# One pool for weights, parts and sums, and a deeper look-ahead in the MLP of a two-layer trunk

## The chip, the cores and the metric

The kernel runs on one core of a Trainium2 chip. The metric is device time in microseconds of one execution, the median of several runs. The engines are called as in the profile: PE (TensorE's matmuls), PEld (its weight loads), DVE (VectorE), ACT (ScalarE), POOL (GpSimd) and SP (SyncE, which here only issues loads and stores). Each engine takes its instructions in the order in which the program has them, and waits on semaphores for the others.

## The reference, cut to what matters

256 tokens of width 2048 go through two layers. Each has attention (main heads and four heads against a memory), an output projection, and a squared-ReLU MLP of width 8192; before the second layer shared keys and values are projected once. Everything is in float32. The change lies in how the weights are brought to TensorE, above all in the MLP:

```python
def sq_relu_mlp(h, g, w_in, w_out):
    return jnp.square(jax.nn.relu(rms_norm(h, g) @ w_in)) @ w_out

def reference(x, mem, ...):
    h = x
    for layer in range(DEPTH):
        ...
        h = h + jnp.concatenate([y_main, y_mem], axis=-1) @ w_o[layer]
        h = h + sq_relu_mlp(h, norm_mlp[layer], w_mlp_in[layer], w_mlp_out[layer])
    return h
```

## The kernel before, in words

**Weights as a stream.** All weights are read once, as a list `stream` of 932 units in the order of their use. A unit is 128 x 1024 float32, 4 KB in each partition. `prepare` (L248) makes one ready: SP loads it into a tile `raw` (L269, L261 or L226), ACT casts it to `hi` in the format fp32r (L189, L265 or L243), and DVE subtracts, `lo = raw - hi` (L192, L266 or L244). TensorE then multiplies with hi and lo apart: hi by hi, hi by lo and lo by hi give a product that is close to float32. `weights` (L273) hands out the next unit, and before that prepares as many as `AHEAD` says: the unit that is handed out and three more.

**Pools.** `raws` has 6 buffers, `his` 4, `los` 5, all of 4 KB in a partition. A fourth pool `grp` has 13 buffers of the same size, for what lives longer: heads, sums, tiles of the residual stream, copies.

**The MLP.** `mlp` (L1022) goes over four chunks of 2048 of the 8192 hidden features, and over the output in column groups. `mlp_steps` writes out the order of work from the table `TURNS`:
- U: one up tile, `features_major` (L408), two units: 16 matmuls of 512 columns with hi and then 16 of 256 columns with lo, into one bank. Then `up` (L1220): ACT copies one half of the bank to `low` (L467), DVE adds the other half (`up`, L1228), and `finish` multiplies by the root (L1210), squares on ACT (L1213) and splits the result into hi and lo (L1160 on ACT, L1161 on DVE) in the tile `hid`. After every second tile of those that a sevenfold product reads, `block_sums` also makes sums of 128x128 blocks on DVE (L1191 to L1194) and splits them into `s_w` and `s_x`.
- S: a sevenfold pair, `Group.seven` (L1130): a 2x2 block product with seven multiplications in place of eight. It takes two loads, left and right, and four units of the stream. Its 21 matmuls of 512 columns go in four steps of 6, 3, 6 and 6, one for each unit; within a product they read hi, lo, hi.
- A and B: direct units, 12 matmuls each.

There are 41 pairs S in a layer, 82 in all, and all but two follow an up tile U at once.

**The four units of a pair.** `prepare_seven` (L220) is called once for each. Step 0 loads both sides and splits the left one. Step 1 splits one block of the right side, half a unit (128x512). Step 2 forms two sums in place on DVE (L238, L239) and splits the right side. Step 3 forms two more (L241, L242) and splits the left side.

**What sets the order.** TensorE's instructions keep the order of the program. Those of ACT, DVE, POOL and SP are put in an order by a scheduler when the kernel is built; it also decides which free buffer of a pool a tile gets. Once built, each engine's order is fixed, and an instruction that waits holds up all that stand behind it on its engine.

Of the kernel before, what the change touches and what calls it, by code (L numbers as in the profile page):

```python
# [9 lines left out]
F32 = mybir.dt.float32  # L10
# [6 lines left out]
P = 128  # L17
# [18 lines left out]

WO_ORDER = [12, 13, 14, 15] + list(range(12))
AHEAD = 3

FIRST = 4  # L40

# [79 lines left out]
def trunk(  # L121
# [17 lines left out]
    nc = Engines(tc)  # L139

    const = ctx.enter_context(tc.tile_pool(name="const", bufs=1))
    raws = ctx.enter_context(tc.tile_pool(name="raws", bufs=6))
    his = ctx.enter_context(tc.tile_pool(name="his", bufs=4))
    los = ctx.enter_context(tc.tile_pool(name="los", bufs=5))
    acts = ctx.enter_context(tc.tile_pool(name="acts", bufs=2))
    grp = ctx.enter_context(tc.tile_pool(name="grp", bufs=13))
    wide = ctx.enter_context(tc.tile_pool(name="wide", bufs=7))
    nar = ctx.enter_context(tc.tile_pool(name="nar", bufs=6))
    tiny = ctx.enter_context(tc.tile_pool(name="tiny", bufs=4))
# [31 lines left out]

    stream = []
    prepared = deque()
    state = {"next": 0}

    def parts(raw, hi, lo, shared=False):

# [6 lines left out]
    def prepare_pair(load, split):  # L194


        i = state["next"]
        state["next"] = i + 2
        units = [
            (  # L200
                stream[n],
                raws.tile([P, 1024], F32, name=f"raw{n}", tag="raw"),
                his.tile([P, 1024], F32R, name=f"hi{n}", tag="hi"),
                los.tile([P, 1024], F32R, name=f"lo{n}", tag="lo"),
            )
            for n in (i, i + 1)
        ]
        for k2 in range(2):
            c = slice(512 * k2, 512 * (k2 + 1))
            load(i + k2)  # L210
            for src, raw, _, _ in units:
                nc.sync.dma_start(raw[:, c], src[:, c])
        for k2 in range(2):
            c = slice(512 * k2, 512 * (k2 + 1))
            split(i + k2)
            for _, raw, hi, lo in units:
                parts(raw[:, c], hi[:, c], lo[:, c], i == 0 and k2 == 0)
        prepared.extend((hi, lo) for _, _, hi, lo in units)

    def prepare_seven(i, seven):  # L220

        if seven.step == 0:
            seven.raw = []
            for n, ap in enumerate(seven.sides):
                raw = raws.tile([P, 1024], F32, name=f"raw{i}_{n}", tag="raw")
                nc.sync.dma_start(raw[:].rearrange("p (o x) -> p o x", o=4), ap)  # L226
                seven.raw.append(raw[:].rearrange("p (o k n) -> p k o n", o=4, k=2))
        left, right = seven.raw
        b11, b21, b12, b22 = left[:, 0], left[:, 1], right[:, 0], right[:, 1]
        hi = his.tile([P, 1024], F32R, name=f"hi{i}", tag="hi")  # L230
        lo = los.tile([P, 1024], F32R, name=f"lo{i}", tag="lo")
        hi4 = hi[:].rearrange("p (k o n) -> p k o n", o=4, k=2)
        lo4 = lo[:].rearrange("p (k o n) -> p k o n", o=4, k=2)
        src = left if seven.step in (0, 3) else right
        if seven.step == 1:
            src, hi4, lo4 = b22, hi4[:, 0], lo4[:, 0]
        elif seven.step == 2:
            nc.vector.tensor_tensor(b22, b22, b12, op=ALU.subtract)  # L238
            nc.vector.tensor_tensor(b12, b12, b11, op=ALU.subtract)  # L239
        elif seven.step == 3:  # L240
            nc.vector.tensor_tensor(b11, b22, b11, op=ALU.add)  # L241
            nc.vector.tensor_tensor(b21, b21, b11, op=ALU.subtract)  # L242
        nc.scalar.copy(hi4, src)  # L243
        nc.vector.tensor_tensor(lo4, src, hi4.bitcast(F32), op=ALU.subtract)  # L244
        seven.step += 1
        prepared.append((hi, lo))

    def prepare():  # L248
        i = state["next"]
        if i >= len(stream):  # L250
            return
        state["next"] = i + 1
        if isinstance(stream[i], Sevenfold):
            prepare_seven(i, stream[i])
            return
        raw = raws.tile([P, 1024], F32, name=f"raw{i}", tag="raw")
        hi = his.tile([P, 1024], F32R, name=f"hi{i}", tag="hi")
        lo = los.tile([P, 1024], F32R, name=f"lo{i}", tag="lo")
        if isinstance(stream[i], Gathered):

            nc.sync.dma_start(raw[:].rearrange("p (o x) -> p o x", o=4), stream[i].ap)  # L261
            turned = raw[:].rearrange("p (o k n) -> p k o n", o=4, k=2)
            hi4 = hi[:].rearrange("p (k o n) -> p k o n", o=4, k=2)
            lo4 = lo[:].rearrange("p (k o n) -> p k o n", o=4, k=2)
            nc.scalar.copy(hi4, turned)  # L265
            nc.vector.tensor_tensor(lo4, turned, hi4.bitcast(F32), op=ALU.subtract)  # L266
            prepared.append((hi, lo))
            return
        nc.sync.dma_start(raw[:], stream[i])  # L269
        parts(raw[:], hi[:], lo[:])  # L270
        prepared.append((hi, lo))

    def weights(held=0):  # L273

        while len(prepared) < AHEAD + 1 - held and state["next"] < len(stream):
            prepare()
        return prepared.popleft()

# [146 lines left out]
    def two_tiles(act, evacuates, order=tuple(range(KT))):  # L425

        banks = [ps_mm.tile([P, 512], F32, name="acc", tag="acc") for _ in range(2)]
        units = [weights(held=i) for i in range(4)]
        kinds = [(wide_ones, 0), (narrow_ones, 1)]
        if width["last"] == "narrow":  # L430
            kinds.reverse()
        for i, (ones_of, part) in enumerate(kinds):
            if i == 1 and part == 1:

                prepare()
            for b in range(2):
                for h in range(2):
                    ones_of(
                        banks[b], units[2 * b + h][part], act, order[8 * h : 8 * h + 8],
                        i == 0 and h == 0, i == 1 and h == 1,  # L440
                    )
                    if i == 1 and len(prepared) < AHEAD + 1:
                        prepare()
                if i == 1:
                    evacuates[b](banks[b])
                slot()
# [575 lines left out]
    def mlp(l, xg_, sq, h, done):  # L1022
# [62 lines left out]
        class Group:  # L1085
# [19 lines left out]
            def add(self, q, a, w):  # L1105
# [13 lines left out]
                    self.staged.append((dst, copy[:]))  # L1119
                else:  # L1120
                    whole, i = place(q, self.n)
                    first = whole.name not in self.copies
                    if first:
                        self.copies[whole.name] = heads4("copy")
                    copy = self.copies[whole.name]
                    nc.scalar.copy(copy[:, i * 512 : (i + 1) * 512], src)  # L1126
                    if not first:
                        nc.gpsimd.dma_start(out=whole[:], in_=copy[:], accum_op=ALU.add)  # L1128
# [73 lines left out]
            return [a11, first[0] if whole else s1, s2, s3, s4]  # L1202

        began = clock["slot"]
        chunks = [({}, {}) for _ in range(NCH)]

        def finish(c, f):
# [50 lines left out]
        for c, n, kind, i in mlp_steps(l):  # L1258
# [19 lines left out]
            else:  # L1278
                groups[c, n].direct(i, "AB".index(kind) + 1)
        c = NCH - 1  # L1280
        start_side(merge_first())

        def down(o, bank):
# [222 lines left out]
```

## Time and profile before

| what | value |
|---|---|
| median of 3 runs | 2206.19 us (2205.29 to 2206.84) |
| the profiled execution's own time | 2207.83 us |
| its span, first to last instruction | 2206.0 us |
| busy: PE, PEld, DVE, ACT, POOL | 98%, 83%, 80%, 59%, 11% |
| first MLP, 460 to 1125 us: PE, DVE, ACT busy | 648.75, 584.89, 413.60 us |
| second MLP, 1510 to 2206 us: PE, DVE, ACT busy | 673.66, 593.92, 421.62 us |
| loads of w_down, w_up, w_in: issue to landing, median | 6.6, 4.5, 3.8 us |

How to read the rows of the profile. A group's row gives the line, the engine, the operation, `out<-in` by the program's names, the shapes and the count, then busy time and the mean of one in ns, then the idle time of the engine just ahead of them and what ended it. A row of the timeline gives start, duration, engine, line and operation, and in brackets the idle time before it with its releaser. A matmul of 512 columns shows as 0.39 us, but the next one starts 0.23 us after it, since they overlap. A row of the windows gives a stretch of time, its length, the busy time of PE, PEld, DVE, ACT and POOL with the count of instructions, the clock that TensorE was granted as a share of the full one, and what the DMA engines did.

### The profile page before, as it was taken

The page shows a single profiled execution, that of the slowest core. Times are in us where ns is not written, and L with a number is a line of the kernel's source. Part 1 is how long each engine was busy: PE and PEld are TensorE (multiplying, and loading weights), DVE is VectorE, ACT ScalarE, POOL GpSimd, SP SyncE. Part 2 cuts the span into 40 slices and gives each one's busy share as a digit, 9 for nine tenths or more (in the row PEclk, how much of TensorE's full clock was granted, in tenths as well). Part 3 has the DMA queues.
Part 4 walks back from the last instruction along what each step waited for, and adds up shares of the span by engine and source line. Part 5 has one row for each costly group of instructions (what it writes and reads, how often), then busy time and mean ns, then how long its engine had stood idle before and what let it go on. Part 6 is the DMA issues. An engine that isn't in the chain of part 4 may idle for free.

```text
span 2206.0 us, 30581 instructions
## 1 busy us (share of the span) xinstructions
PE 2163.0 (98%) x11002; PEld 1837.8 (83%) x11002; DVE 1759.5 (80%) x2637; ACT 1295.6 (59%) x1932; POOL 241.9 (11%) x275
## 2 busy tenths in 40 slices
PE   9999999999999999999999999999999999999999
PEld 8888888887887887887878888888788788888787
DVE  7778886679889898897985556567989989888886
ACT  7644445556666665666545446655666566666653
POOL 0110103500000000000050112361000000000000
PEclk9999999999999999999999999999999999999999
DMA  9655556656665867867757663566676576776874
GB/s 331 209 162 186 177 176 207 213 174 192 196 212 173 238 197 215 238 209 231 218 173 210 183 198 118 153 211 191 172 216 190 185 227 203 221 216 213 245 213 124
DMA packets 220809, 441.94 MB, mean 200 GB/s; under 512 B 14065, under 2 KB 145137, under 8 KB 220657
## 3 DMA queue, kind: packets, MB, share of 16 engines
q1 hardware_dynamic: 212592, 410.63, 60.4%
q0 software_dynamic: 7488, 27.27, 5.0%
q8 instruction: 86, 1.41, 0.3%
q10 hardware_dynamic: 576, 2.10, 0.3%
q14 instruction: 67, 0.54, 0.1%
HBM read 415.82 MB, written 7.34 MB: 192 GB/s over the span
## 4 chain that ended last, share of the span: by engine, by line
PE 85%; DMA 7%; DVE 5%; ACT 2%; issue 1%; SPq 0%; ACTq 0%
PE acc L92 80%; DMA raw<-in_w_down 6%; DVE lo L244 2%; PE yp L92 1%; PE accs L92 1%; PE tp L92 1%; ACT hi L243 1%; PE s L92 1%; PE z L92 1%; ACT hi L265 1%; DVE lo L192 0%; DVE raw L242 0%; DVE raw L241 0%; ACT copy L1126 0%; DVE raw L239 0%
## 5 line engine op out<-in xcount | busy, mean ns | idle before, releaser
L192 DVE TENSOR_TENSOR lo<-raw,hi 128x1024 fp32r<-128x1024 f32 (+1 forms) x524 | 640.5, 1237 | 192.7 <-ACT hi L189 168.4
L189 ACT CAST hi<-raw 128x1024 fp32r<-128x1024 f32 (+1 forms) x524 | 539.2, 1045 | 302.7 <-PE acc L92 248.6
L92 PE MATMUL acc<-mlpx,hi 128*128 128x512 f32 x2048 | 485.3, 390 | 0.0
L243 ACT CAST hi<-raw 128x1024 fp32r<-128x1024 f32 x328 | 309.1, 944 | 280.9 <-DVE raw L239 153.3
L92 PE MATMUL acc<-hi,hid 128*128 128x512 f32 x1308 | 452.2, 393 | 3.8 <-ACT hi L243 2.4
L92 PEld LDWEIGHTS acc<-mlpx,hi 128*128 128x128 f32 x2048 | 384.3, 188 | 80.4 <-DVE up L1228 0.3
L244 DVE TENSOR_TENSOR lo<-raw,hi 128x1024 fp32r<-128x1024 f32 x328 | 354.1, 1087 | 93.3 <-ACT hi L243 90.1
L92 PEld LDWEIGHTS acc<-hi,hid 128*128 128x128 f32 x1308 | 247.2, 189 | 55.2 <-ACT hi L243 4.8
L92 PE MATMUL acc<-lo,hid 128*128 128x512 f32 x654 | 258.7, 396 | 14.8 <-DVE lo L244 14.8
L92 PEld LDWEIGHTS acc<-mlpx,lo 128*128 128x128 f32 x2048 | 261.5, 191 | 9.2
L92 PE MATMUL acc<-mlpx,lo 128*128 128x256 f32 x2048 | 264.9, 283 | 0.0
L92 PE MATMUL acc<-hi,xg 128*128 128x512 f32 x640 | 208.5, 398 | 0.0
L92 PEld LDWEIGHTS acc<-lo,hid 128*128 128x128 f32 x654 | 123.8, 189 | 42.6 <-DVE lo L244 21.2
L92 PEld LDWEIGHTS acc<-hi,xg 128*128 128x128 f32 x640 | 120.2, 188 | 24.6
L1128 POOL DMA_DIRECT2D e<-copy x16 | 13.8, 862 | 1021.1 <-ACT copy L1126 1019.7
L92 PE MATMUL acc<-lo,xg 128*128 128x512 f32 x320 | 124.8, 390 | 0.6 <-DVE lo L192 0.6
L92 PE MATMUL acc<-hi,s_w 128*128 128x512 f32 x328 | 121.2, 407 | 2.0 <-ACT hi L243 2.0
L467 ACT COPY low<-acc 128x256 f32<-128x256 f32 x188 | 69.4, 369 | 88.1 <-PE acc L92 86.8
L92 PE MATMUL acc<-y,hi 128*128 128x512 f32 x512 | 119.9, 391 | 0.0
L266 DVE TENSOR_TENSOR lo<-raw,hi 128x1024 fp32r<-128x1024 f32 x84 | 102.9, 1236 | 16.9 <-ACT hi L265 16.1
L265 ACT CAST hi<-raw 128x1024 fp32r<-128x1024 f32 x84 | 88.3, 1059 | 39.0 <-PE acc L92 33.6
L92 PEld LDWEIGHTS acc<-y,hi 128*128 128x128 f32 x512 | 95.0, 188 | 19.0
(232 smaller groups left out, 2775.9 us busy)
## 6 DMA issues: line engine op xcount, KB each, us to landing
raw<-in_w_up SPq DMA_DIRECT2D x256, 512.0 KB, 4.5
raw<-in_w_down SPq DMA_DIRECT2D x256, 512.0 KB, 6.6
raw<-in_w_in SPq DMA_DIRECT2D x80, 512.0 KB, 3.8
raw<-in_w_o SPq DMA_DIRECT2D x64, 512.0 KB, 4.2
raw<-in_w_mem SPq DMA_DIRECT2D x28, 512.0 KB, 5.8
raw<-in_w_kv_v SPq DMA_DIRECT2D x24, 512.0 KB, 4.3
raw<-in_w_kv_k SPq DMA_DIRECT2D x24, 512.0 KB, 4.4
raw<-in_w_q SPq DMA_DIRECT2D x24, 512.0 KB, 4.3
```

Of the source, the lines that this page charges most:

```text
L92: return self._tc.keep_in_program_order(fn(*args, **kwargs))
L189: nc.scalar.copy(hi[:, :n], raw[:, :n])
L192: nc.vector.tensor_tensor(lo, raw, hi.bitcast(F32), op=ALU.subtract)
L243: nc.scalar.copy(hi4, src)
L244: nc.vector.tensor_tensor(lo4, src, hi4.bitcast(F32), op=ALU.subtract)
L265: nc.scalar.copy(hi4, turned)
L266: nc.vector.tensor_tensor(lo4, turned, hi4.bitcast(F32), op=ALU.subtract)
L467: nc.scalar.copy(low[:], bank[:, T:])
L1128: nc.gpsimd.dma_start(out=whole[:], in_=copy[:], accum_op=ALU.add)
```

## The change

Three things. The three pools `raws`, `his` and `los` are given up, and `grp` grows from 13 to 28 buffers, the same memory (6 + 4 + 5 + 13): any unit's raw, hi or lo, and any sum or copy, takes any buffer that is free. In the MLP, up to its last chunk's direct part, `weights` keeps four units ahead in place of three. And in `prepare_seven` the two sums of step 3 are formed in step 2, behind the first two. The lines of the changed file are up to three lower than before (L243 becomes L240, L244 L241, L467 L464, L1228 L1227, L238 to L242 become L236 to L239). A fourth edit only changes the key of a dictionary from a tile's name to the tile itself.

```diff
+AHEAD_MLP = 4
...
-    raws = ctx.enter_context(tc.tile_pool(name="raws", bufs=6))
-    his = ctx.enter_context(tc.tile_pool(name="his", bufs=4))
-    los = ctx.enter_context(tc.tile_pool(name="los", bufs=5))
     acts = ctx.enter_context(tc.tile_pool(name="acts", bufs=2))
-    grp = ctx.enter_context(tc.tile_pool(name="grp", bufs=13))
+    grp = ctx.enter_context(tc.tile_pool(name="grp", bufs=28))
...
-    state = {"next": 0}
+    state = {"next": 0, "ahead": AHEAD}
...
-        raw = raws.tile([P, 1024], F32, name=f"raw{i}", tag="raw")
-        hi = his.tile([P, 1024], F32R, name=f"hi{i}", tag="hi")
-        lo = los.tile([P, 1024], F32R, name=f"lo{i}", tag="lo")
+        raw = grp.tile([P, 1024], F32, name=f"raw{i}", tag="g4")
+        hi = grp.tile([P, 1024], F32R, name=f"hi{i}", tag="g4")
+        lo = grp.tile([P, 1024], F32R, name=f"lo{i}", tag="g4")
...
         elif seven.step == 2:
             nc.vector.tensor_tensor(b22, b22, b12, op=ALU.subtract)
             nc.vector.tensor_tensor(b12, b12, b11, op=ALU.subtract)
-        elif seven.step == 3:
             nc.vector.tensor_tensor(b11, b22, b11, op=ALU.add)
             nc.vector.tensor_tensor(b21, b21, b11, op=ALU.subtract)
...
-        while len(prepared) < AHEAD + 1 - held and state["next"] < len(stream):
+        while len(prepared) < state["ahead"] + 1 - held and state["next"] < len(stream):
...
         began = clock["slot"]
+        state["ahead"] = AHEAD_MLP
...
         c = NCH - 1
+        state["ahead"] = AHEAD
         start_side(merge_first())
```

The change also gives the scheduler other buffers to work with, so the order on the engines moves. Two places show it, both for one pair in the first MLP, units 188 to 191 of the stream, which follows the up tile of units 186 and 187. `low` and `up` are that up tile's last steps and read its finished bank (`acc`).

DVE before, from the lo of the pair's first unit (188) to that of the fourth (191):

```order
L244 TENSOR_TENSOR lo188_5126<-raw188_0_5121,hi188_5125 128x1024
L244 TENSOR_TENSOR lo189_5137<-raw188_1_5123,hi189_5136 128x512
L238 TENSOR_TENSOR raw188_1_5123<-raw188_1_5123 128x4x128
L239 TENSOR_TENSOR raw188_1_5123<-raw188_1_5123,raw188_0_5121 128x4x128
L241 TENSOR_TENSOR raw188_0_5121<-raw188_1_5123,raw188_0_5121 128x4x128
L242 TENSOR_TENSOR raw188_0_5121<-raw188_0_5121 128x4x128
L244 TENSOR_TENSOR lo190_5181<-raw188_1_5123,hi190_5180 128x1024
L1228 TENSOR_TENSOR up_5174<-acc_5135,low_5172 128x256
L244 TENSOR_TENSOR lo191_5187<-raw188_0_5121,hi191_5186 128x1024
```

DVE now, the same stretch:

```order
L241 TENSOR_TENSOR lo188_5111<-raw188_0_5106,hi188_5110 128x1024
L1227 TENSOR_TENSOR up_5173<-acc_5130,low_5171 128x256
L241 TENSOR_TENSOR lo189_5121<-raw188_1_5108,hi189_5120 128x512
L1209 SCALAR_TENSOR_TENSOR up_5173<-up_5173,ri_mlp0_4400 128x256
L236 TENSOR_TENSOR raw188_1_5108<-raw188_1_5108 128x4x128
L237 TENSOR_TENSOR raw188_1_5108<-raw188_1_5108,raw188_0_5106 128x4x128
L1159 TENSOR_TENSOR hid0_4166<-up_5173,hid0_4166 128x256
L238 TENSOR_TENSOR raw188_0_5106<-raw188_1_5108,raw188_0_5106 128x4x128
L239 TENSOR_TENSOR raw188_0_5106<-raw188_0_5106 128x4x128
L241 TENSOR_TENSOR lo190_5132<-raw188_1_5108,hi190_5131 128x1024
L241 TENSOR_TENSOR lo191_5180<-raw188_0_5106,hi191_5179 128x1024
```

`up` has moved from behind the third unit's lo to a place ahead of the second unit's, and with it the four sums and three lo now stand behind it.

ACT before, from the hi of unit 188 to that of unit 191:

```order
L243 CAST hi188_5125<-raw188_0_5121 128x1024
L243 CAST hi189_5136<-raw188_1_5123 128x512
L243 CAST hi190_5180<-raw188_1_5123 128x1024
L467 COPY low_5172<-acc_5135 128x256
L243 CAST hi191_5186<-raw188_0_5121 128x1024
```

ACT now:

```order
L240 CAST hi188_5110<-raw188_0_5106 128x1024
L464 COPY low_5171<-acc_5130 128x256
L240 CAST hi189_5120<-raw188_1_5108 128x512
L1212 ACTIVATE up_5173<-up_5173 128x256
L1158 CAST hid0_4166<-up_5173 128x256
L240 CAST hi190_5131<-raw188_1_5108 128x1024
L240 CAST hi191_5179<-raw188_0_5106 128x1024
```

The copy `low` has moved from behind the third unit's hi to a place ahead of the second unit's. Of the 82 pairs, 76 stand like this now, `low` ahead of the second hi and `up` ahead of the second lo; in the other kinds the steps of `block_sums` lie between the sums too. Before, the `up` of the tile just ended stood ahead of no second lo; at 12 pairs it stood ahead of the third lo, among the sums.

More of the change, by code (lines that the diff above doesn't have):

```diff
@@ L201, in prepare_pair @@
                 stream[n],
-                raws.tile([P, 1024], F32, name=f"raw{n}", tag="raw"),
-                his.tile([P, 1024], F32R, name=f"hi{n}", tag="hi"),
-                los.tile([P, 1024], F32R, name=f"lo{n}", tag="lo"),
+                grp.tile([P, 1024], F32, name=f"raw{n}", tag="g4"),
+                grp.tile([P, 1024], F32R, name=f"hi{n}", tag="g4"),
+                grp.tile([P, 1024], F32R, name=f"lo{n}", tag="g4"),
             )
@@ L224, in prepare_seven @@
             for n, ap in enumerate(seven.sides):
-                raw = raws.tile([P, 1024], F32, name=f"raw{i}_{n}", tag="raw")
+                raw = grp.tile([P, 1024], F32, name=f"raw{i}_{n}", tag="g4")
                 nc.sync.dma_start(raw[:].rearrange("p (o x) -> p o x", o=4), ap)
@@ L255, in prepare @@
             return
-        raw = raws.tile([P, 1024], F32, name=f"raw{i}", tag="raw")
-        hi = his.tile([P, 1024], F32R, name=f"hi{i}", tag="hi")
-        lo = los.tile([P, 1024], F32R, name=f"lo{i}", tag="lo")
+        raw = grp.tile([P, 1024], F32, name=f"raw{i}", tag="g4")
+        hi = grp.tile([P, 1024], F32R, name=f"hi{i}", tag="g4")
+        lo = grp.tile([P, 1024], F32R, name=f"lo{i}", tag="g4")
         if isinstance(stream[i], Gathered):
@@ L441, in two_tiles @@
                     )
-                    if i == 1 and len(prepared) < AHEAD + 1:
+                    if i == 1 and len(prepared) < state["ahead"] + 1:
                         prepare()
@@ L1121, in add @@
                     whole, i = place(q, self.n)
-                    first = whole.name not in self.copies
+                    key = id(whole)
+                    first = key not in self.copies
                     if first:
-                        self.copies[whole.name] = heads4("copy")
-                    copy = self.copies[whole.name]
+                        self.copies[key] = heads4("copy")
+                    copy = self.copies[key]
                     nc.scalar.copy(copy[:, i * 512 : (i + 1) * 512], src)
```

## The prediction

> **What bounds the kernel now.** I read the page first, then the busy time by stage, the waits of TensorE, and at last the timeline around a pair of weight units that waits.
>
> ```profile
> PE 2163.0 (98%) x11002; PEld 1837.8 (83%) x11002; DVE 1759.5 (80%) x2637; ACT 1295.6 (59%) x1932; POOL 241.9 (11%) x275
> ...
> 460.00:1125.00 665.00, 648.75 (x3268) 547.79 (x3267) 584.89 (x851) 413.60 (x611) 24.78 (x29) 0.99 0.70 207
> ...
> 1510.00:2206.00 696.00, 673.66 (x3411) 569.19 (x3409) 593.92 (x861) 421.62 (x621) 18.96 (x24) 0.99 0.67 201
> ...
> PE acc L92 <- DVE lo L244: 23.1, 27, 1.6
> PE acc L92 <- ACT hi L243: 9.1, 13, 2.7
> ```
>
> The first row is busy time over the whole span: TensorE is the bound, and idle for 43 us of the 2206. The next two are the two MLPs (span, then busy PE, PEld, DVE, ACT, POOL): 16.3 and 22.3 of those 43 us lie there, while DVE is busy for 88% and 85%. The last two say for what: 40 waits, 32.2 us, for the two halves of the weights of the sevenfold pairs (L243 and L244; a pair is four units of the stream). So time can only be won or lost at one question: are the hi and lo of a pair's four units ready when TensorE comes to them?
>
> A pair that waits, with its rows on TensorE, ACT and DVE in turn (start, duration, last the idle time and its releaser):
>
> ```profile
> 501.94 0.40 PE L92 MATMUL acc<-hi,hid 128*128 128x512 f32 x1
> 502.17 0.40 PE L92 MATMUL acc<-lo,hid 128*128 128x512 f32 x1
> ...
> 504.01 0.39 PE L92 MATMUL acc<-hi,hid 128*128 128x512 f32 x1
> 505.09 0.50 PE L92 MATMUL acc<-lo,hid 128*128 128x512 f32 x1 [0.70 <-DVE lo L244]
> ...
> 506.14 0.40 PE L92 MATMUL acc<-hi,s_w 128*128 128x512 f32 x1
> 506.78 0.50 PE L92 MATMUL acc<-hi,s_w 128*128 128x512 f32 x1 [0.24 <-ACT hi L243]
> 508.04 0.50 PE L92 MATMUL acc<-lo,s_w 128*128 128x512 f32 x1 [0.76 <-DVE lo L244]
> ```
>
> ```profile
> 502.14 0.37 ACT L467 COPY low<-acc 128x256 f32<-128x256 f32 x1 [1.00 <-PE acc L92]
> 502.41 1.05 ACT L243 CAST hi<-raw 128x1024 fp32r<-128x1024 f32 x1
> ...
> 505.68 1.05 ACT L243 CAST hi<-raw 128x1024 fp32r<-128x1024 f32 x1 [1.32 <-DVE raw L242]
> ```
>
> ```profile
> 502.55 0.42 DVE L1228 TENSOR_TENSOR up<-acc,low 128x256 f32<-128x256 f32 x1 [0.60 <-ACT low L467]
> 502.89 0.68 DVE L241 TENSOR_TENSOR raw<-raw,raw 128x512 f32<-128x512 f32 x1
> 503.49 0.42 DVE L1210 SCALAR_TENSOR_TENSOR up<-up,ri_mlp 128x256 f32<-128x256 f32 x1
> 503.82 1.22 DVE L244 TENSOR_TENSOR lo<-raw,hi 128x1024 fp32r<-128x1024 f32 x1
> 504.96 0.68 DVE L242 TENSOR_TENSOR raw<-raw 128x512 f32<-128x512 f32 x1
> ...
> 506.76 1.23 DVE L244 TENSOR_TENSOR lo<-raw,hi 128x1024 fp32r<-128x1024 f32 x1 [1.11 <-ACT hi L243]
> ```
>
> The pair's first matmul starts at 501.94. ACT's copy `low` reads the bank of the up tile just ended, so it can't start before 502.14, and in ACT's queue the cast hi of the pair's third unit stands behind it. On DVE, `up` waits for `low`, and the third unit's lo stands behind `up`. From there it is a chain: third unit's lo, last weight sum, fourth hi, fourth lo. TensorE loses 0.86, 0.41 and 1.03 us (starts 1.08, 0.64 and 1.26 apart, where the step is 0.23): 2.30 us. A pair that doesn't wait looks like this on DVE, and its first matmul:
>
> ```profile
> 570.97 0.69 DVE L244 TENSOR_TENSOR lo<-raw,hi 128x512 fp32r<-128x512 f32 x1 [1.07 <-ACT hi L243]
> 571.69 0.69 DVE L238 TENSOR_TENSOR raw<-raw 128x512 f32<-128x512 f32 x1
> 572.42 0.69 DVE L239 TENSOR_TENSOR raw<-raw,raw 128x512 f32<-128x512 f32 x1
> 573.15 0.69 DVE L241 TENSOR_TENSOR raw<-raw,raw 128x512 f32<-128x512 f32 x1
> 573.87 0.69 DVE L242 TENSOR_TENSOR raw<-raw 128x512 f32<-128x512 f32 x1
> 574.48 2.50 DVE L244 TENSOR_TENSOR lo<-raw,hi 128x1024 fp32r<-128x1024 f32 x2
> ...
> 575.17 0.40 PE L92 MATMUL acc<-hi,hid 128*128 128x512 f32 x1
> ```
>
> All four sums are done before 575.17: nothing of them stands behind the up tile's end. That is the rule before; the waiting pair is the exception.
>
> **The change, part by part.** The pool and the fourth unit ahead remove buffer waits (hi of four buffers: a cast had to wait until TensorE let go of the unit four back). The new order shows what the scheduler made of it: the pair's first unit is split earlier, but the half-size hi of the second now stands behind `low` on ACT, its lo behind `up` on DVE, and all four sums, the third and fourth hi and lo behind these. In the order of DVE I counted the 82 pairs: 76 stand so, in three kinds by what lies between. Plain (46 pairs): only the up tile's own steps. With block sums (22): also four steps of 128x128 and splits of 128x256. With block sums in the last chunk (8): the same with one split less. The six others differ.
>
> The durations for the sum, beside those above:
>
> ```profile
> L243 ACT CAST hi<-raw 128x512 fp32r<-128x512 f32 x82 | 51.0, 622 | 30.1 <-PE acc L92 20.0 <-DMA raw<-in_w_down 6.7 <-issue 1.2
> ...
> 487.42 0.28 DVE L1192 TENSOR_TENSOR up<-up 128x128 f32<-128x128 f32 x1
> 487.62 0.69 DVE L239 TENSOR_TENSOR raw<-raw,raw 128x512 f32<-128x512 f32 x1
> ```
>
> So: a cast of half size 0.62, of full size 1.05; DVE is free 0.60 after a 128x512 (502.89 to 503.49) and 0.73 where the next needs its result (571.69 to 572.42), 0.33 after a 128x256 (503.49 to 503.82), 0.20 after a 128x128 (487.42 to 487.62), 1.14 after a full lo (503.82 to 504.96); from one engine's end to the next one's start 0.05. Take the pair's first matmul as 0; `low` starts at 0.20, `up` at 0.61, as above.
>
> Plain: hi 2 on ACT 0.47 to 1.09; DVE `up` to 0.95, lo 2 from 1.12 to 1.80, the multiplication to 2.05, two sums to 3.47; hi 3 from 3.52 to 4.57; the split of hid and the other two sums keep DVE until 5.04; lo 3 to 6.26; hi 4 5.17 to 6.22; lo 4 to 7.48. TensorE wants lo 2 at 1.59, gets it at 1.84: 0.25. It wants hi 3 at 2.29, gets it at 4.62: 2.33. Lo 3, wanted at 4.85, comes at 6.31: 1.46. Lo 4, at 7.52, is in time. Sum 4.0 us.
>
> With block sums: two sums end at 3.58, hi 3 is there at 4.73; splits and block steps put lo 3 at 5.15 to 6.37; the fourth sum ends at 7.31, hi 4 at 8.41, lo 4 at 9.67. Lost: 0.30, 2.39, 1.46, 0.90, 1.03, sum 6.1. With one split less and the fourth sum right behind lo 3: 5.4. The six others I put at 3. Together 46 x 4.0 + 22 x 6.1 + 8 x 5.4 + 6 x 3 = 379 us. The same sum for the pair at 501.94 gives 2.46 where the rows show 2.30, so the low end is 0.93 of it, 354. Nothing hides this: the next up tile needs TensorE, ACT's next `low` waits for that tile's end, so each pair starts from the same place again. DVE's and ACT's spare time, now larger, lies behind the pair, where it helps only the next up tile.
>
> Gone are the 40 waits: 32.2 us, and 0.16 each for the matmul that doesn't overlap its predecessor (0.39 long, 0.23 apart): 39 us.
>
> The two last sums one unit sooner: four 128x512 operations either way. In the plain kind they delay lo 3 by two of them; this is in the sum.
>
> The clock needs rows of its own (stretch, busy PE, PEld, DVE, ACT, POOL, clock):
>
> ```profile
> core 0: 2206.0 us, clock 0.995
> ...
> 529.60:533.00 3.40, 2.39 (x10) 1.62 (x10) 3.02 (x3) 3.40 (x5) 0.00 (x0) 1.00 0.58 171
> ...
> 850.45:853.86 3.41, 1.78 (x7) 1.05 (x6) 3.41 (x6) 2.73 (x4) 0.00 (x0) 1.00 0.00 0
> 853.87:857.27 3.40, 3.40 (x9) 2.67 (x8) 3.40 (x4) 1.89 (x4) 0.00 (x0) 0.50 0.76 271
> ```
>
> After 3.41 us with PE busy for 1.78 the next 3.4 us were granted half the clock, with 16 matmul slots for 9 matmuls; after 3.40 with 2.39 busy they weren't. The mean of 0.995 is 11 us lost now. In a plain pair TensorE stands from 2.29 to 6.31 but for one matmul, so a window that lies well inside costs half of 3.41 us behind it. Bounds: none, 0; one at each pair, 82 x 1.7 = 140. I take the middle, 70, since many windows straddle the wait's ends, and in the block-sum kind the slow window falls on further waits. In the row that set it off all idle time together is 1.6 us. The Trainium skill, "TensorE: Matmul & The Clock Gate", on HAM oscillation, puts the rule as no idle gaps over about 3.4 us. By that rule no wait here would slow the clock, and the sum would be lower by the 70; this trace differs, with 1.6 us of idle and a clock of 0.50 behind them.
>
> Elsewhere: in the new order 14 units outside the pairs stand close behind work that waits for TensorE: eleven lo behind an evacuation, and three loads of w_in that SP issues behind a head's bias load, which waits for DVE. Bounds 0 and one lo (1.22) each, 17; I take 17. At the eight chunk changes loads may land late besides: up to 30 us, in the high end only.
>
> The sum: the profiled execution's own 2207.8, less 39 and 11, plus 379, 70 and 17: 2624; the median of the three runs is 1.6 lower: **2622 us**. Its own bounds: 2207.8 - 50 + 354 = 2512, and 2207.8 - 50 + 379 + 140 + 17 + 30 = 2724.
>
> **The rivals.**
> *Faster*: the first unit of a pair is split about 3 us sooner, and if hi 2 and lo 2 were done before the up tile ends, all 40 waits would go, and most slow windows: 2207.8 - 39 - 11 = 2158. It decides where hi 2 stands against `low` on ACT: ahead, it wins. The order says behind; for it speaks only that ACT and DVE have idle time. 4%.
> *No change*: the new waits come, but short enough to be covered by what the old 40 give back, under 0.5 us a pair. Lo 3 then would have to be there 2.8 us after the pair's start; at 501.94, with less ahead of it, it took 3.1. 2%.
> *Smaller*: each pair pays no more than the waiting pair does now, 2.30, and the clock holds, as it did there: 2207.8 - 50 + 189 + 17 = 2364. Against it: two more sums and a half unit stand in the chain. 7%.
> *Clock*: each pair brings two slow windows, both full of matmuls: 2207.8 - 50 + 379 + 280 + 17 = 2834. For it: PE is idle for more of each window than the 1.6 us that sufficed at 850.45. 7%.
>
> **How the numbers follow.** The forecast has 80%. Its bounds, widened by 40 us on both sides for the kinds of pair that I did not work one by one, give 2470 to 2760; the four rivals, 20%, lie outside. A difference of 0.2% (4.4 us) is about what a measurement of this kernel can tell. Slower: the forecast and two rivals, 94%; faster 4%; within 0.2% 2%.
>
> **What would show it.** Right: PE busy falls well under 98%, waits for the pairs' hi and lo of some 320 us or more at nearly all 82 pairs, three to five at each; on ACT hi 2 starts 0.3 us after `low`; idle DVE behind each pair; granted clock under 0.98. A step is wrong if lo 3 of a plain pair comes under 4 us after the pair's start, if the block-sum kind loses no more than the plain one, or if the clock stays at 0.99. The whole is wrong if ACT's casts of the second unit start before `low`.

## The result and the profile after

The changed kernel takes 2865.51 us (median of 4 runs, 2864.82 to 2869.52) against 2205.74 for the kernel before in the same session (2203.74 to 2206.84): a ratio of 1.2996, 95% interval 1.2974 to 1.3019. It is slower, as forecast, but by 660 us where 416 were forecast, and above the range's upper end.

The page's row of busy time, the mean clock, and TensorE's three largest waits of the changed kernel (us in total, times, the longest):

```profile
PE 2471.3 (86%) x11002; PEld 1968.8 (69%) x11002; DVE 1752.0 (61%) x2637; ACT 1274.6 (45%) x1932; POOL 214.5 (7%) x275
...
core 0: 2863.9 us, clock 0.903
...
PE acc L93 <- ACT hi L240: 164.0, 96, 2.1
PE acc L93 <- DVE lo L241: 105.7, 128, 1.2
PE acc L93 <- DVE lo L190: 71.2, 45, 4.4
```

The same 11002 matmuls keep TensorE busy 308 us longer (2471.3 against 2163.0), at a mean clock of 0.903 against 0.995, and it is idle for 393 us in place of 43. The first two waits are for the pairs' hi and lo (L240 and L241 are L243 and L244 of before): 269.7 us in 224 waits where there were 32.2 us in 40. The third, for lo at L190, belongs to ordinary units and was hardly there before.

The time by stage shows where it went. The stretches are cut at the first use of units 164, 456, 614 and 906, so that the second and the fourth row are the two stretches of pairs (columns: stretch, length, busy PE, PEld, DVE, ACT, POOL, clock, and the DMA's share and GB/s). First before, then after:

```profile
0.00:491.60 491.60, 488.98 (x2424) 414.55 (x2425) 373.14 (x700) 272.68 (x424) 85.83 (x95) 1.00 0.64 205
491.60:1075.00 583.40, 567.94 (x2851) 478.72 (x2850) 510.67 (x732) 368.03 (x540) 15.90 (x20) 0.99 0.70 209
1075.00:1545.80 470.80, 468.22 (x2527) 406.92 (x2526) 312.84 (x409) 256.07 (x390) 121.17 (x136) 1.00 0.60 181
1545.80:2130.80 585.00, 568.11 (x2850) 478.94 (x2849) 511.31 (x732) 369.03 (x540) 16.00 (x20) 0.99 0.70 209
2130.80:2206.00 75.20, 69.75 (x358) 58.62 (x357) 51.54 (x67) 29.80 (x38) 2.96 (x4) 1.00 0.53 154
```

```profile
0.00:586.60 586.60, 522.95 (x2424) 433.55 (x2425) 370.71 (x700) 263.95 (x424) 69.80 (x95) 0.95 0.51 172
586.60:1415.10 828.50, 691.27 (x2851) 528.79 (x2849) 504.68 (x725) 366.41 (x540) 15.27 (x19) 0.86 0.52 145
1415.10:1945.10 530.00, 490.19 (x2525) 417.00 (x2526) 314.17 (x416) 247.56 (x391) 109.66 (x137) 0.97 0.54 164
1945.10:2773.60 828.50, 691.26 (x2851) 528.63 (x2849) 504.74 (x725) 366.19 (x540) 15.44 (x19) 0.86 0.52 145
2773.60:2863.90 90.30, 75.58 (x357) 60.85 (x357) 57.67 (x73) 30.50 (x39) 4.38 (x5) 0.96 0.49 146
```

The pairs' stretches cost 245.1 and 243.5 us more, 488.6 together; the three others 95.0, 59.2 and 15.1, 169.3 together. In each stretch of pairs TensorE is busy 123 us longer with the same work: most of that is the clock of 0.86. The forecast had 400 us for the pairs (379 and 70, less the 39 of the old waits and the 10 us of slow clock that lay there) and 16 for the rest (17 less 1).

A plain pair of the changed kernel, the one whose order was shown above (units 188 to 191), on TensorE, ACT and DVE:

```profile
650.18 0.40 PE L93 MATMUL acc<-hi,hid 128*128 128x512 f32 x1
...
651.57 0.39 PE L93 MATMUL acc<-hi,s_x 128*128 128x512 f32 x1
652.06 0.50 PE L93 MATMUL acc<-lo,s_x 128*128 128x512 f32 x1
652.40 0.40 PE L93 MATMUL acc<-hi,s_x 128*128 128x512 f32 x1
654.80 0.70 PE L93 MATMUL acc<-hi,hid 128*128 128x512 f32 x1 [2.00 <-ACT hi L240]
656.52 0.80 PE L93 MATMUL acc<-lo,hid 128*128 128x512 f32 x1 [1.02 <-DVE lo L241]
657.12 0.63 PE L93 MATMUL acc<-hi,hid 128*128 128x512 f32 x1
657.54 0.63 PE L93 MATMUL acc<-hi,s_w 128*128 128x512 f32 x1
```

```profile
650.38 0.37 ACT L464 COPY low<-acc 128x256 f32<-128x256 f32 x1 [8.02 <-PE acc L93]
650.65 0.63 ACT L240 CAST hi<-raw 128x512 fp32r<-128x512 f32 x1
...
653.70 1.04 ACT L240 CAST hi<-raw 128x1024 fp32r<-128x1024 f32 x1 [0.47 <-DVE raw L237]
655.36 1.04 ACT L240 CAST hi<-raw 128x1024 fp32r<-128x1024 f32 x1 [0.62 <-DVE raw L239]
```

```profile
650.79 0.42 DVE L1227 TENSOR_TENSOR up<-acc,low 128x256 f32<-128x256 f32 x1 [6.60 <-ACT low L464]
651.31 0.69 DVE L241 TENSOR_TENSOR lo<-raw,hi 128x512 fp32r<-128x512 f32 x1
...
655.25 2.42 DVE L241 TENSOR_TENSOR lo<-raw,hi 128x1024 fp32r<-128x1024 f32 x2
```

The chain is the forecast's to a few hundredths: counted from 650.18, hi 2 runs from 0.47 to 1.10 (forecast 0.47 to 1.09), lo 2 starts at 1.13 (1.12), hi 3 at 3.52 (3.52), lo 3 at 5.07 (5.04), hi 4 at 5.18 (5.17); TensorE gets hi 3 at 4.62 (4.62) and lo 3 at 6.34 (6.31). At a step of 0.23 it loses 0.26, 2.17 and 1.49 us, 3.9 where 4.0 was forecast. ACT's 8.02 us and DVE's 6.60 us of idle time ahead of `low` and `up` show that the splitting engines had time and stood behind the up tile's end. What the forecast had too small comes after: after 656.52 the matmuls start up to 0.60 apart, then 0.43, in place of 0.23. The clock of those windows:

```profile
651.52:654.93 3.41, 1.30 (x5) 0.45 (x4) 3.34 (x7) 1.87 (x3) 0.00 (x0) 1.00 0.66 195
654.93:658.34 3.41, 2.39 (x5) 1.56 (x6) 3.41 (x4) 2.98 (x4) 0.00 (x0) 0.50 0.01 3
658.34:661.76 3.42, 3.42 (x9) 2.64 (x8) 2.73 (x3) 0.91 (x1) 0.00 (x0) 0.50 0.39 95
```

The first window, with TensorE busy for 1.30 us, brings a slow second one. In that one TensorE still waits (for lo 3), and a slow third follows. In the whole trace there are 99 stretches at half the clock, 64 of two windows (6.83 us) and 35 of one (3.41), 555.5 us together; before there were 6, 23.1 us together. In the two stretches of pairs lie 450.6 of the 555.5 us now, and 20.5 of the 23.1 before.

### The profile page after: what moved, and what is told of

The parts are those of the page before. It is cut to its first block, busy times and chain, and to the rows that moved or that the text cites. A ratio compares the mean times of both kernels' runs of the same rounds, so it can differ in the third digit from the quotient of the medians.

```text
span 2863.9 us, 29997 instructions
## 1 busy us (share of the span) xinstructions
PE 2471.3 (86%) x11002; PEld 1968.8 (69%) x11002; DVE 1752.0 (61%) x2637; ACT 1274.6 (45%) x1932; POOL 214.5 (7%) x275
## 4 chain that ended last, share of the span: by engine, by line
PE 57%; DVE 21%; ACT 5%; issue 2%; POOL 1%; DMA 0%; SPq 0%; ACTq 0%; DVEq 0%
PE acc L93 55%; DVE lo L241 6%; ACT hi L240 2%; DVE raw L239 2%; DVE raw L238 2%; DVE raw L237 2%; DVE raw L236 2%; ACT low L464 1%; DVE lo L190 1%; DVE up L1209 1%; DVE hid L1159 1%; ACT hi L187 1%; DVE lo L263 1%; POOL low L1011 1%; PE z L93 1%
## 5 line engine op out<-in xcount | busy, mean ns | idle before, releaser
L190 DVE TENSOR_TENSOR lo<-raw,hi 128x1024 fp32r<-128x1024 f32 (+1 forms) x524 | 630.1, 1227 | 129.0 <-ACT hi L187 127.2
L93 PE MATMUL acc<-hi,hid 128*128 128x512 f32 x1308 | 507.6, 434 | 141.7 <-ACT hi L240 141.5
L187 ACT CAST hi<-raw 128x1024 fp32r<-128x1024 f32 (+1 forms) x524 | 527.8, 1038 | 61.4 <-DMA raw<-in_w_in 24.3
L93 PE MATMUL acc<-mlpx,hi 128*128 128x512 f32 x2048 | 517.6, 407 | 0.9
L464 ACT COPY low<-acc 128x256 f32<-128x256 f32 x188 | 69.9, 372 | 858.4 <-PE acc L93 858.0
L93 PEld LDWEIGHTS acc<-hi,hid 128*128 128x128 f32 x1308 | 275.4, 211 | 227.3 <-ACT hi L240 172.9
L1227 DVE TENSOR_TENSOR up<-acc,low 128x256 f32<-128x256 f32 x128 | 54.3, 424 | 572.2 <-ACT low L464 572.2
L241 DVE TENSOR_TENSOR lo<-raw,hi 128x1024 fp32r<-128x1024 f32 x328 | 355.8, 1088 | 41.4 <-ACT hi L240 36.9
L93 PE MATMUL acc<-lo,hid 128*128 128x512 f32 x654 | 297.4, 455 | 89.3 <-DVE lo L241 79.0
L240 ACT CAST hi<-raw 128x1024 fp32r<-128x1024 f32 x328 | 308.2, 940 | 141.2 <-DVE raw L239 78.1
L93 PE MATMUL acc<-hi,s_w 128*128 128x512 f32 x328 | 185.4, 606 | 3.5 <-ACT hi L240 3.5
L93 PEld LDWEIGHTS acc<-hi,s_w 128*128 128x128 f32 x328 | 100.7, 307 | 39.7 <-ACT hi L240 16.5
L93 PE MATMUL acc<-lo,s_w 128*128 128x512 f32 x164 | 104.2, 635 | 12.9 <-DVE lo L241 12.9
```

The costliest lines, as they stand in the source:

```text
L93: return self._tc.keep_in_program_order(fn(*args, **kwargs))
L187: nc.scalar.copy(hi[:, :n], raw[:, :n])
L190: nc.vector.tensor_tensor(lo, raw, hi.bitcast(F32), op=ALU.subtract)
L464: nc.scalar.copy(low[:], bank[:, T:])
L1227: nc.vector.tensor_tensor(t[:], bank[:, :T], low[:], op=ALU.add)
```

## The experiments

Two theories were to be told apart first. A: the shared pool costs time through the order that the scheduler makes with it (the steps of a pair behind the up tile's end), and the clock does the rest. B: buffers or loads come late on the chip, whatever the order. Beside them, which of the three edits it is. Edits are shown against the changed kernel where nothing else is said, cut (`...`) to the lines that matter. Every experiment that took over 2400 us was run once, the others 4 to 11 times.

**The edits apart.** First the pool alone.

```diff
-AHEAD_MLP = 4
+AHEAD_MLP = 3
...
             nc.vector.tensor_tensor(b12, b12, b11, op=ALU.subtract)
+        elif seven.step == 3:
             nc.vector.tensor_tensor(b11, b22, b11, op=ALU.add)
```

> The pool of 28 buffers alone: three units ahead as before, the last two sums back in step 3. Theory A (the shared pool makes the scheduler put the up tile's low and up ahead of the pair's second hi and lo, and the waits and the slow clock follow from that order): the order has low ahead of the second hi at 74 of the 82 pairs, so nearly the whole slowdown is here, 2750 to 2950 us, granted clock about 0.90. Rival B (the fourth unit ahead, or the sums, starve something else): 2200 to 2300 us, clock 0.99.

Measured: 2851.68 us, clock 0.912, stretches of pairs 825.0 and 821.7 us. Against the 2203.79 of the kernel before in the same session the pool alone costs 648 us, nearly the whole slowdown. Then the fourth unit ahead alone, on the kernel before:

```diff
+AHEAD_MLP = 4
...
+        state["ahead"] = AHEAD_MLP
```

> The fourth unit ahead in the MLP alone, with the three pools of before. Theory A: no pair has low ahead of its second hi, and 8 in place of 12 have it ahead of the third, so four pairs lose their 2.4 us of waits: 2190 to 2206 us. Rival B (the look-ahead takes buffers that others need): over 2250 us.

Measured: 2196.86 us, ratio 0.9966 (0.9956 to 0.9977). The waits for the pairs' hi and lo are 27.3 us in 38 times, where they were 32.2 in 40. This edit gains 7 us (against 2203.79). The third one, the two sums one unit sooner, moves no instruction on any engine when it is put into the kernel before by itself; the built program is the same but for the numbers in tile names, so it has no run of its own.

**What must not be shared.** The change, with the loads in 6 buffers of their own and 22 for the rest:

```diff
-    grp = ctx.enter_context(tc.tile_pool(name="grp", bufs=28))
+    raws = ctx.enter_context(tc.tile_pool(name="raws", bufs=6))
+    grp = ctx.enter_context(tc.tile_pool(name="grp", bufs=22))
...
-                raw = grp.tile([P, 1024], F32, name=f"raw{i}_{n}", tag="g4")
+                raw = raws.tile([P, 1024], F32, name=f"raw{i}_{n}", tag="raw")
```

> The changed kernel with one part undone: the loads have their own 6 buffers again, and hi, lo, sums and copies share 22. Four units ahead, early sums as in the change. Theory A, with the finding that in the shared pool a load waits for the buffer that TensorE has just let go while the hi and lo of units ahead hold theirs: the pairs' second to fourth hi now stand ahead of low nearly everywhere, so most of the 40 waits of before go as well: 2140 to 2195 us, clock 1.00. Rival B (sharing buffers between weights and sums, or the fourth unit ahead, is what costs): 2400 us or more.

Measured: 2196.57 us, ratio 0.9970 (0.9961 to 0.9979), stretches 577.5 and 576.8 us. So hi, lo, sums and copies may share one pool without harm. The time is just above the expected one, and TensorE's waits say why:

```profile
PE acc L93 <- DVE up L1228: 19.3, 14, 3.9
PE acc L93 <- DVE lo L242: 5.4, 9, 0.8
```

The waits for hi and lo are nearly gone, but a new one took their place: here the splits run so far ahead that `up` stands behind them on DVE, and TensorE waits for the bank that `up` has to read. The opposite division has raw, hi and lo together in 15 buffers and the rest in its old 13 (the sums back in step 3):

```diff
+    wts = ctx.enter_context(tc.tile_pool(name="wts", bufs=15))
-    grp = ctx.enter_context(tc.tile_pool(name="grp", bufs=28))
+    grp = ctx.enter_context(tc.tile_pool(name="grp", bufs=13))
```

> A pool of 15 buffers for raw, hi and lo together, sums and copies apart in 13 as before; four units ahead, sums in step 3. Theory A (it is loads that share with hi and lo): low stands ahead of the second hi at 78 of 82 pairs, so as slow as the changed kernel or slower, 2800 to 3000 us, clock about 0.90. Rival C (sums and copies in the pool, whose buffers come free only after POOL's slow adding transfers, hold up the loads): about 2200 us.

Measured: 2884.03 us, clock 0.908. The longer-lived tiles and POOL's transfers aren't needed for it: loads that share a pool with hi and lo are enough.

**The order, forced in the change.** The pairs' steps, `low` and `up` are kept in the order of the program text on ACT and DVE, in the same shared pool:

```diff
-        nc.scalar.copy(hi4, src)
-        nc.vector.tensor_tensor(lo4, src, hi4.bitcast(F32), op=ALU.subtract)
+        pin(nc.scalar.copy(hi4, src))
+        pin(nc.vector.tensor_tensor(lo4, src, hi4.bitcast(F32), op=ALU.subtract))
```

> The change whole, but in the MLPs the casts, sums and lo of the pairs, the copy `low` and the addition `up` keep the order of the program text on ACT and DVE; so the pair's second and third hi stand ahead of `low` again, the fourth 3.5 us of TensorE's work behind it. Same pools, same loads, same buffers. Order theory (the pool costs time only through the order it gave the engines): the first chain of waits goes, each MLP's stretch of pairs falls from 828 us to 580 to 640, the clock rises to 0.96 or more, and since the stages outside the MLPs keep their new order (+80 to +169 us) the whole takes 2300 to 2500 us. Rival (buffers come free late, so that loads or casts really wait on the chip, whatever the order): the stretches stay over 750 us and the whole over 2750.

Measured: 2523.47 us, clock 0.962, stretches 670.5 and 669.4 us. That is 342 us off the change with the same buffers and loads, and far under theory B's 2750. It stays above what A said, and the rows show what is left (TensorE at one pair, then ACT):

```profile
624.74 0.51 PE L93 MATMUL acc<-hi,s_w 128*128 128x512 f32 x1 [0.28 <-ACT hi L241]
```

```profile
621.07 0.38 ACT L465 COPY low<-acc 128x256 f32<-128x256 f32 x1 [0.52 <-PE acc L93]
...
623.65 1.04 ACT L241 CAST hi<-raw 128x1024 fp32r<-128x1024 f32 x1
```

The fourth hi (623.65) still stands behind `low` and the up tile's other steps, since the program text has it there. I had given it little, and it is the wait that remains at this pair, with that for its lo. It isn't all: in this kernel TensorE waits 142.0 us, in 161 waits, for the pairs' hi and lo, and followed back row by row 24 of them (21.5 us) end at a load or at a transfer of `e`, a tile of the same pool. For those theory B isn't excluded.

**The order, forced in the kernel before.** The reverse: the old pools, but the pairs' second and third unit are held back behind `up` and keep that place.

```diff
+        if step and in_mlp["hold"]:
+            held_back.append(ops)
+        else:
+            ops()
...
             nc.vector.tensor_tensor(t[:], bank[:, :T], low[:], op=ALU.add)
+            behind_up()
```

> The kernel before with its separate pools, its three units ahead and its sums where they were; only the order in the MLPs is forced: the casts, sums and lo of a pair's second and third unit are held back until the addition `up` of the tile just ended, and keep their place behind it (as at 76 pairs of the change; here at 80). No buffer is shared. Order theory (the pool cost time only by the order it gave): each stretch of pairs goes from 583 to between 770 and 840 us, with the clock in them near that of the change, and the rest stays as before: 2580 to 2720 us in all, 2690 the likeliest. Rival (the order is a symptom, and what costs is the buffers' coming free): with the old pools the time stays under 2300.

Measured: 2867.67 us, stretches 907.1 and 907.8 us, the rest 1051 against 1038 before. With no buffer shared, the order alone costs 666 us (against 2201.81 in the same session): as the reason of what the pairs lose in the change, theory B isn't needed. It cost more in the pairs than the change, which I had not expected. The difference in the order is the place of the last two sums: kept in the order of the old program text, which forms them in step 3, they stand behind the third unit's lo, and the fourth hi and lo come later than in the change. So the same kernel with the change's third edit added:

```diff
                 pin(nc.vector.tensor_tensor(b12, b12, b11, op=ALU.subtract))
-            elif step == 3:
                 pin(nc.vector.tensor_tensor(b11, b22, b11, op=ALU.add))
```

> The kernel of e9_late_order (old pools, the pairs' second and third unit held back behind `up`), with the change's third edit added: the two last sums stand ahead of the third unit's lo in place of behind it. The order of a plain pair on DVE and ACT is then that of the change but for one place (the multiplication by the root ahead of the second lo). If the order alone makes the pairs' loss, the stretches of pairs fall from 907 us to what the change has, 815 to 845, and the whole to 2690 to 2740: the change's time less what its order costs outside the MLPs. If e9 was slower than the change for another reason than the place of the two sums, the stretches stay over 880 and the whole over 2820.

Measured: 2723.48 us. The two stretches of pairs, beside 828.50 in the change:

```profile
491.80:1331.00 839.20, 677.25 (x2850) 532.43 (x2849) 521.87 (x729) 377.85 (x542) 15.88 (x20) 0.86 0.48 146
...
1807.90:2645.10 837.20, 675.54 (x2850) 531.10 (x2849) 521.72 (x729) 377.81 (x542) 16.17 (x20) 0.86 0.48 146
```

With the old pools and the change's order (but for one place, and at 80 pairs in place of 76) the pairs lose about what they lose in the change, the clock of 0.86 included. And the sums that stand one unit sooner, worth nothing by themselves, are worth 144 us (2867.67 less 2723.48) once the pair stands behind the up tile.

**The clock.** Matmuls of no use fill the two long waits of a pair, 82 x 14 of them:

```diff
                     w = weights()
+                    if step == 2:
+                        self.fill(j, 9)
...
+                        gap = (lambda: self.fill(j, 5)) if step == 2 and k2 == 0 else None
+                        self.add(q, a, part(w, k2), gap)
```

> The change whole, but TensorE is given matmuls of no use where it waits in a pair: nine of 512 columns ahead of the third unit's first product and five between that product's hi and lo halves (2.04 and 1.14 us at 0.227 each, under the 2.33 and 1.46 of the forecast's waits). They add products into one of the pair's sums, so the output isn't the reference's. Clock theory (TensorE's idle time in a pair, over about 2.1 us of a 3.41-us window, halves the clock of the next window, and the slow window's own idle time that of the one behind it): the half-clock stretches leave most plain pairs, the granted clock rises from 0.90 to 0.96 or more, each stretch of pairs falls from 828 to about 730 us and the whole to about 2670 (2620 to 2720), although TensorE is given 82 x 14 x 0.227 = 261 us more of work. Rival (the waits themselves are longer than priced and the clock is only read off them): the time stays at 2860 or rises.

Measured: 2726.18 us, clock 0.982: 139 us faster than the change with 261 us more work for TensorE, and 6 us above the upper end that I had written. The stretches of pairs by windows, and a pair (`neg_tri_r` are the fillers):

```profile
591.20:1350.00 758.80, 729.41 (x3411) 570.43 (x3409) 504.82 (x725) 367.09 (x540) 15.28 (x19) 1.00 0.60 159
...
1878.10:2635.20 757.10, 728.86 (x3410) 570.29 (x3408) 504.76 (x724) 367.02 (x540) 15.47 (x19) 1.00 0.60 159
```

```profile
673.32 0.40 PE L93 MATMUL acc<-hi,hid 128*128 128x512 f32 x1
...
675.75 2.26 PE L93 MATMUL acc<-hid,neg_tri_r 128*128 128x512 f32 x9
677.94 0.50 PE L93 MATMUL acc<-hi,hid 128*128 128x512 f32 x1
678.28 1.33 PE L93 MATMUL acc<-hid,neg_tri_r 128*128 128x512 f32 x5
679.65 0.50 PE L93 MATMUL acc<-lo,hid 128*128 128x512 f32 x1
```

The third unit's hi comes 4.62 us after the pair's start and its lo 6.33 after, as in the change: the chain on ACT and DVE is the same. But no window in the pairs is slow any more (the clock is 1.00, and the trace has no half-clock stretch in them), and so each stretch is 70 us shorter. The clock is a cost of its own, and its cause is TensorE's idle time in the pair.

**Outside the MLPs.** The kernel with the forced order in the pairs (2523.47), and the same now for ordinary units and for the output projection's evacuations (an evacuation is the way of a finished bank through copy, additions and scaling):

```diff
-        nc.scalar.copy(hi[:, :n], raw[:, :n])
+        pin(nc.scalar.copy(hi[:, :n], raw[:, :n]))
...
-            nc.vector.tensor_tensor(r, bank[:, :T], low2[:], op=ALU.add)
+            pin(nc.vector.tensor_tensor(r, bank[:, :T], low2[:], op=ALU.add))
```

> The kernel of e5_pinned (the change, with the pairs' steps in the order of the program text), and now outside the MLPs too the casts and lo of a unit, the copy `low` and the last addition of the output projection keep that order on ACT and DVE. In the two output projections (units 112 to 144 and 562 to 594) the lo of six units of which the change puts 1.1 to 2.0 us of TensorE's work behind an evacuation then has 4.9 us or more. Theory (outside the MLPs too it is the order: weights behind a long evacuation through ACT, POOL and DVE): these two stages go from 117.9 and 115.2 us to 95 to 100, and the whole from 2523 to about 2480. Rival (the waits there come from buffers or loads): they stay over 110 us.

Measured: 2491.08 us; the two output projections take 103.8 and 101.0 us, where the change had 117.9 and 115.6 and the kernel before 94.6 and 94.0. They get back 14.1 of 23.3 and 14.6 of 21.6 us, so in these stages most of it is the order; they stay 1 to 4 us over the expected 100, and the whole 11 over the expected 2480. The stretches outside the pairs together take 1146.5 us here, 1207.0 in the change and 1037.6 before: for the other 109 us no experiment shows the cause.

**Better than both.** Two versions of the kernel before, with four units ahead. One moves a buffer from the rest to hi (6, 5, 5 and 12):

```diff
-    his = ctx.enter_context(tc.tile_pool(name="his", bufs=4))
+    his = ctx.enter_context(tc.tile_pool(name="his", bufs=5))
...
-    grp = ctx.enter_context(tc.tile_pool(name="grp", bufs=13))
+    grp = ctx.enter_context(tc.tile_pool(name="grp", bufs=12))
```

> The kernel before with its separate pools, one of the 28 buffers moved: 6 raw, 5 hi, 5 lo, 12 for the rest, and four units ahead in the MLP. Order theory: 6 of 82 pairs have the third hi behind `low`, where the kernel before has 12, so most of the 40 old waits (39 us) and the 11 us of slow clock go: 2165 to 2197 us. Rival (what was gained with four units ahead alone, 2197, is all there is, since the last buffer of the rest is then missed): 2195 to 2215.

Measured: 2181.37 us, ratio 0.9898 (0.9882 to 0.9915), clock 0.998. Its largest waits:

```profile
PE acc L93 <- DVE up L1230: 10.4, 7, 2.0
PE acc L93 <- DVE lo L245: 5.3, 10, 1.0
```

The other shares hi and lo alone, in 9 buffers:

```diff
-    his = ctx.enter_context(tc.tile_pool(name="his", bufs=4))
-    los = ctx.enter_context(tc.tile_pool(name="los", bufs=5))
+    wts = ctx.enter_context(tc.tile_pool(name="wts", bufs=9))
```

> The kernel before with four units ahead in the MLP, and hi and lo alone in one pool of 9 buffers; raw keeps its 6 and the rest its 13. What is shared are tiles with the same life, from cast to last matmul. Theory (sharing harms where a raw, which takes a buffer that TensorE is just letting go of, shares with hi and lo, which take theirs long ahead): 8 of 82 pairs have the third hi behind `low`, the time is 2180 to 2205 us. Rival (any sharing does it): over 2400.

Measured: 2183.35 us, ratio 0.9911 (0.9896 to 0.9925). Both beat both kernels, by some 20 us against the one before; between them the intervals don't decide. Sharing hi and lo, tiles of the same life, does no harm; what of the gain comes from the fourth unit ahead (2196.86 alone) and what from the pool isn't separated further.

## Why the prediction was right in direction and too small

**The order and its chain: right.** The order alone makes the loss in the pairs (with the old pools and the change's order: 839 and 837 us a stretch), the chain runs to the forecast's hundredths, and PE busy, ACT's hi 2 right behind `low`, the idle DVE and the clock under 0.98 came as listed. The block-sum kind loses more than the plain one, as said: about 7.1 against 6.2 us, slow clock included, summed over the starts of the pairs' matmuls.

**The term of 379: about the right size.** With the waits filled, where the clock holds, the stretches of pairs take 1515.9 us against 1168.4 before: 347.5 more. The forecast without its clock term had 379 - 39 - 10 = 330. If the fillers themselves hold TensorE a little, 347.5 is an upper end, and what is put down to the clock below a lower one. In the changed kernel the profile shows only 269.7 us of these waits, under the 320 that I had named as a sign, and 224 waits, 2.7 a pair in place of three to five: at half clock TensorE comes later to the fourth unit and to the next wait, so slow matmuls fill time that it would have waited. Followed back row by row, all 224 waits go through the copy `low` of the up tile just ended, at most 9.6 us earlier, and none ends at a load.

**The clock, 70: the first step that failed.** The prediction put the upper bound at "one at each pair, 82 x 1.7 = 140" and took its middle. One window at each pair was no upper bound: of the 78 slow stretches in the pairs 54 are of two windows, since a slow window that itself holds a wait brings the next. (A window of 3.41 us has 15 slots at the step of 0.23, not the prediction's 16; no term rests on that.) By record the pairs lost 225 us of TensorE's full-speed work (half of 450.6 us). What it cost in time is less, for the reason just given: 1657.0 us of pairs in the change less 1515.9 with the waits filled, 141. So the term was half of what it is, and the wrong bound's own value lies near it by chance. The rival *Clock* had the mechanism, two windows at each pair, but took both to be full of matmuls and none of it to be hidden. Its 280 for the pairs is too much, and its 2834 came near the measured time because it left out what follows.

**Elsewhere, 17: the second step that failed, and the larger one.** The prediction counted 14 units behind work that waits for TensorE and gave each at most one lo, 1.22. The three stretches outside the pairs lost 169.3 us. TensorE is idle there for 107.5 us more than before, and 71.2 us of that are its 45 waits for lo at L190, 1.6 on the mean and up to 4.44. One of the longest, in the first output projection, on TensorE, ACT, POOL and DVE:

```profile
495.43 3.75 PE L93 MATMUL acc<-y,lo 128*128 128x256 f32 x16 [4.43 <-DVE lo L190]
```

```profile
489.04 0.35 ACT L464 COPY low<-acc 128x256 f32<-128x256 f32 x1
492.25 0.51 ACT L476 ACTIVATE mlpx<-h,sm 128x256 fp32r<-128x256 f32 x1 [2.85 <-DVE h L1012]
492.66 3.87 ACT L187 CAST hi<-raw 128x1024 fp32r<-128x1024 f32 x4
```

```profile
488.67 1.52 POOL L496 TENSOR_TENSOR sq<-h 128x256 f32<-128x256 f32 x1 [0.54 <-DVE h L1012]
490.27 0.80 POOL L497 TENSOR_TENSOR mlpsq<-mlpsq,sq 128x256 f32<-128x256 f32 x1
491.04 0.71 POOL L1011 TENSOR_TENSOR low<-low,h 128x256 f32<-128x256 f32 x1
```

```profile
491.79 0.42 DVE L1012 TENSOR_TENSOR h<-acc,low 128x256 f32<-128x256 f32 x1 [1.31 <-POOL low L1011]
...
493.72 4.96 DVE L190 TENSOR_TENSOR lo<-raw,hi 128x1024 fp32r<-128x1024 f32 x4 [0.45 <-ACT hi L187]
```

The cast stands behind the scaling `mlpx`, that waits for DVE's `h`, and that for POOL's addition (L1011). The addition had its `low` from 489.39 on, but stood behind POOL's squares of the tile before (L496, L497) until 491.04. What a unit pays there is the whole evacuation and the lo behind it, with what else stands in the queues of three engines, and not one lo. Followed back row by row, 12 of the 45 waits (30.0 us) go through the output projection's addition like this one and 10 (14.9 us) through another `low`; two (1.1 us) end at a load. The other 21 (25.3 us) stand behind other work, 15 of them ahead of the first output projection, in the attention. And the clock came on top: 103 us of half clock lie in the three stretches, 0.5 before, by record 51 of the 169 us. The prediction counted too few units, and took its bound from the last link of the chain alone.

The sum of it, forecast and measured: pairs at full clock +330 and +347, the pairs' clock +70 and +141, elsewhere +16 and +169; together +416 and +657, the difference of the two spans. In what the pairs lose, late loads had no part that the runs show: the change's order without its pool makes the pairs take 1676.4 us, no less than the change's 1657.0, and ACT's casts in the pairs wait for sums and little for loads:

```profile
L240 ACT CAST hi<-raw 128x1024 fp32r<-128x1024 f32 x328 | 308.2, 940 | 141.2 <-DVE raw L239 78.1 <-DVE raw L237 48.4 <-DMA raw<-in_w_down 14.8
```

What stays open is the rule by which the scheduler comes to this order once loads share buffers with hi and lo. That a load there takes a buffer that TensorE has only just let go of, while hi and lo take theirs long ahead, was read from the built order and is argued, not shown; shown is only which sharing does it: raw with hi and lo, not hi and lo with each other or with the rest. Raw with the rest alone was not run.

## What to carry to other kernels

A change of buffers is a change of order: compare where each engine's instructions stand before pricing anything, and price a step behind an evacuation by the whole chain from the bank to the step, on every engine that it passes. Here a pool shared by tiles of the same life did no harm (hi and lo, with four units ahead: 0.9911), and one shared by loads and what is made of them cost 29% and more. Where waits leave TensorE idle for 1.6 us or more of a window of 3.4, price a slow window behind it, and a second one if further waits of 0.6 us or more fall into the first.

## What the runs showed of the hardware

- The slow clock renews itself. A window of 3.41 us with TensorE busy for 1.30 us was followed by one at 0.50; that one, busy for 2.39 us of slow matmuls, by another at 0.50, while before the same 2.39 us at full clock (529.60) were followed by no slow one. The whole trace of the changed kernel, cut into windows of 3.41 us as its slow stretches lie, shows the same: of the 100 full-speed windows with TensorE idle for 1.6 us or more 97 are followed by a slow one, of the other 575 one is. Of the 162 slow windows all 64 with 0.6 us or more of idle time are followed by another slow one, and none of the other 98.
- No single gap has to be long. In the two stretches of pairs no wait for a hi or lo of a pair is longer than 2.1 us, and 78 stretches at half the clock begin there. The rule cited ahead of the result (the Trainium skill, "TensorE: Matmul & The Clock Gate", on HAM oscillation: no idle gaps over about 3.4 us) is kept by every wait in the pairs, and wasn't enough. The same page of the Trainium skill, in the section "A second HAM failure mode: psum-queue depth-cycling", tells of a kernel whose frequent short idle times between groups of matmuls made the clock oscillate; with this the trace agrees, with 555.5 us at 0.50.
- Work of no use can be faster than none: 261 us of fillers made the kernel 139 us faster (2726.18 against 2865.51).
